# A two-layer hybrid trunk: w_ada sums, bias adds and half-tile norms put at other places of the queues

## The chip, the cores and the metric

One core of one Trainium2 chip runs the whole kernel in one launch. The metric is the device time of an execution in microseconds (us). Five engines take part, each with a queue of its own that it works through in order: TensorE (PE, matrix products), VectorE (DVE), ScalarE (ACT), GpSimd (POOL) and SyncE (SP, which here only issues loads and stores).

## The reference

Two layers of a shared trunk over 256 context tokens and 256 latent tokens, width 1024. Per layer:

```python
sh1, sc1, gt1, sh2, sc2, gt2 = split(silu(c) @ w_ada[l] + b_ada[l], 6)      # for latent and for context
h = rms_norm(x, g_attn[l]) * (1 + sc1) + sh1
p = h @ w_in[l]                                  # gates 2048 | c_q 768 | c_kv 256 | k_r 32 | NA q, k, v 3 x 512
mq = rms_norm(c_q, g_qa) @ w_uq[l]               # 8 heads x 96
kv = rms_norm(c_kv, g_kva) @ w_ukv[l]            # 8 heads x (64 + 64)
mq, mk = rms_norm(mq, g_mq), rms_norm([k_nope, k_r], g_mk)   # and a 2-D rope on 32 of the 96 for latent tokens
y_mla = softmax(mq mk^T / sqrt(96)) v            # context and latent keys
y_na = neighbourhood attention (window, position bias rpb) + context keys, one softmax
y = (sigmoid(g_a) * (y_mla @ w_mla_o) + sigmoid(g_b) * (y_na @ w_na_o)) @ w_out
x = x + gt1 * y
h2 = rms_norm(x, g_mlp[l]) * (1 + sc2) + sh2
x = x + gt2 * (relu(h2 @ w_ff1[l]) ** 2 @ w_ff2[l])
```

Context tokens read only context tokens; in the last layer only the latent stream goes on past the mixer. All is float32; the output is the latent stream.

## The kernel before, in words

**Products in three passes.** Every weight tile and every activation is split into a high part that the fast matmul takes exactly and a low rest. `wsplit` (L124) does it for weights: SP loads a raw tile of 512 KB (`wraw`, L116, five buffers "raw"), ACT writes `whi` (L127), DVE writes `wlo` as raw minus whi (L128); three buffers of each. `mm3` (L100) then gives three matmuls a product: hi x hi (L101), and the two mixed ones (L102, L103). `proj_a` (L131) makes an output tile of 128 features by up to 512 tokens out of 8 slices of depth, 24 matmuls; `proj_b` (L553) makes token tiles, two tokens blocks at a time, in a pair of banks. PSUM banks are A (2), B (3), C (2) and D (1).

**Modulation.** The six vectors of `w_ada` are needed by two streams (latent, context) and no matmul makes them: `ada_side` (L233) loads a slice of 128 rows by 1024 columns, multiplies it by one number of silu(c) per row and adds it to an accumulator on DVE, once per stream (L246 the first slice, L248 the other seven), then transposes and reduces (L259, L260), and one small matmul and four adds (L266, L270) finish it. A generator yields after each slice, and `step(n)` (L165) takes n slices wherever the kernel's author has put a call. `ada(l, j)` is vector j of layer l; j = 2 is the first gate, 3 and 4 shift and scale of the MLP norm, 5 its gate. Here (0, 2) is made beside w_uq, (0, 4) and (0, 3) beside the neighbourhood chunks and the attention behind them, the rest beside the MLP of layer 0.

**Stages of a layer**, in the order of PE's queue: the latent products c_q and c_kv with their norms; w_uq in three blocks of heads (288, 288 and 192 columns, L715 copies, L597 squares); w_ukv in two (L732, L733); the first gates (`gates`); MLA attention head by head; six chunks `chunk_na` (L959) for the neighbourhood q, k and v; neighbourhood attention with more gates between; the branch products and their merge (L1041 gates, L1045 and L1047 m and its low part, on POOL for six of eight tiles); w_out (`last_product`, L1068); the MLP in groups of eight tiles, `ff1` (L1137) and `ff2` (L1177). The norm between two stages is `rms_a` (L306: a matmul with ones, DVE's ms L316, POOL's rt L177), `rms_b` (L321: the factors spread over a bank, L324) and `norm_apply` (L330: per slice u on DVE L334, the high part on ACT L338, the low on DVE L340). `proj_tail` (L150) makes the last tiles before a norm in two halves, one per stream, so that the first half's norm runs under the second.

**Small statistics.** `q_stat` and `k_stat` (L692, L705) turn sums of squares into factors on POOL, for one block of 128 tokens at a time; the position bias comes with four small loads per table on SP (L809) and an add of the window mask on POOL (L810).

**Order.** The code records all of it in one order; a list scheduler of the language then gives each engine a fixed list by its own estimate of times and by the order of the program, and marks such as `keep_in_program_order` pin single instructions. What an engine's list says is therefore fixed before the run.

Of the kernel before, what the change touches and what calls it, by code (L numbers as in the profile page):

```python
# [45 lines left out]
def trunk(ctx: ExitStack, tc, t):
# [186 lines left out]
    def ada_side(parts, acc):  # L233


        for l, j, zs in parts:
            accs = [acc(z) for z in zs]
            for k in range(KD):
                raw = wraw(t["w_ada"][l], k, 1, j * D, D)[:, 0]
                for z, tiles in zip(zs, accs):  # L240
# [216 lines left out]
    for l in range(DEPTH):  # L457
# [149 lines left out]
        def rope(z, tab, lt, n):  # L607
# [8 lines left out]
            for i in range(2):  # L616
                nc.gpsimd.tensor_tensor(out=zz[:, :, :, i], in0=aa[:, :, :, i], in1=bb[:, :, :, 1 - i], op=ALU.add)
# [63 lines left out]
        if l == 0:  # L681
# [3 lines left out]
            step(2)  # L685
# [616 lines left out]
```

## Time and profile before

| what | us |
|---|---|
| median of 3 runs | 1317.86 (1313.06 to 1319.54) |
| the profiled execution | 1316.76 |
| its span, first to last instruction | 1315.0 |
| PE busy | 1276.4 (97%) |
| weight loads into PE | 1094.9 (83%) |
| DVE busy | 903.5 (69%) |
| ACT busy | 582.6 (44%) |
| POOL busy | 269.7 (21%) |
| mean granted clock of PE | 0.992 of 2.4 GHz |

The busy time of PE counts from a matmul's start to its modelled end, and neighbours overlap. In a timeline row the columns are start, duration, engine, line, operation, output tile <- input tiles, shapes, how many in a row, and in brackets the idle time just before it with what ended it. The shares hide where a stage waits; for that the gaps of PE are read one by one.

### The profile page before, as it was taken

To read this page: it belongs to the slowest core of one execution; us is meant where nothing else is said; L and a number is where in the kernel's file an instruction comes from. 1 tells how busy PE (TensorE), PEld (TensorE's weight loads), DVE (VectorE), ACT (ScalarE), POOL (GpSimd) and SP (SyncE) were. 2 spreads that over 40 slices of the span, in tenths; PEclk is the share of its full clock that TensorE was granted. 3 is DMA by queue.
4 is the path that set the end of the run, shared out by engine and by line. 5 is a ranking of instruction groups with operands and counts; after the bars stand their busy time and mean duration, and the time that the engine had idled before them with its cause. 6 is when DMAs were issued, how large, how long until landed. Compare 5 with 4: busy or idle time off the path is not lost.

```text
span 1315.0 us, 20278 instructions
## 1 busy us (share of the span) xinstructions
PE 1276.4 (97%) x7783; PEld 1094.9 (83%) x7783; DVE 903.5 (69%) x1545; ACT 582.6 (44%) x1052; POOL 269.7 (21%) x283
## 2 busy tenths in 40 slices
PE   7989999999999999999999999989999999999997
PEld 5788888986787898888888888889889789999896
DVE  4588387758985597997775665756763967665553
ACT  4445376446423334322323313455654545554452
POOL 0325501421004003210201100038122112121011
PEclk9999999999999999999999999999999999999999
DMA  9865500544495336566675572476214657656652
GB/s 290 298 147 148 174 17 17 180 134 57 114 321 182 114 111 179 169 182 195 205 224 176 160 224 85 120 176 182 77 49 113 134 171 211 175 159 194 192 183 90
DMA packets 241857, 208.01 MB, mean 158 GB/s; under 512 B 24464, under 2 KB 220816, under 8 KB 241376
## 3 DMA queue, kind: packets, MB, share of 16 engines
q1 hardware_dynamic: 231728, 190.16, 50.3%
q10 hardware_dynamic: 9520, 16.29, 3.5%
q8 instruction: 61, 1.00, 0.3%
q0 software_dynamic: 512, 0.27, 0.1%
q14 instruction: 36, 0.29, 0.1%
HBM read 195.15 MB, written 11.53 MB: 157 GB/s over the span
## 4 chain that ended last, share of the span: by engine, by line
PE 55%; DVE 3%; DMA 2%; ACT 1%; POOL 1%; issue 1%; POOLq 0%; ACTq 0%; DVEq 0%
PE psB L101 7%; PE psB L103 7%; PE psB L102 7%; PE psA L103 6%; PE psA L101 6%; PE psA L102 6%; PE psC L103 4%; PE psC L101 4%; PE psC L102 4%; PE psC L865 1%; DVE wlo L128 1%; PE psD L885 1%; ACT whi L127 1%; DMA raw<-in_w_uq_dram 1%; DMA bias<-in_rpb_dram 1%
## 5 line engine op out<-in xcount | busy, mean ns | idle before, releaser
L128 DVE TENSOR_TENSOR wlo<-raw,whi 128x1024 fp32r<-128x1024 f32 (+3 forms) x252 | 308.5, 1226 | 190.9 <-ACT whi L127 185.4
L127 ACT ACTIVATE whi<-raw 128x1024 fp32r<-128x1024 f32 (+3 forms) x252 | 260.4, 1035 | 364.1 <-PE psB L102 113.8
L248 DVE SCALAR_TENSOR_TENSOR ada<-raw,silu,ada 128x1024 f32<-128x1024 f32 (+1 forms) x126 | 153.1, 1245 | 25.5 <-DMA raw<-in_w_ada_dram 25.2
L102 PE MATMUL psA<-wlo,h 128*128 128x256 f32 (+2 forms) x408 | 121.1, 297 | 2.5 <-DVE wlo L128 2.5
L101 PE MATMUL psA<-whi,h 128*128 128x256 f32 (+2 forms) x408 | 120.8, 296 | 1.2 <-ACT h L338 1.1
L103 PE MATMUL psA<-whi,h 128*128 128x256 f32 (+2 forms) x408 | 120.9, 296 | 0.0
L101 PE MATMUL psB<-h,whi 128*128 128x512 f32 (+1 forms) x288 | 99.1, 345 | 0.1
L103 PE MATMUL psB<-h,wlo 128*128 128x512 f32 (+1 forms) x288 | 99.0, 344 | 0.0
L102 PE MATMUL psB<-h,whi 128*128 128x512 f32 (+1 forms) x288 | 99.0, 344 | 0.0
L101 PE MATMUL psA<-h,whi 128*128 128x512 f32 (+1 forms) x248 | 87.8, 355 | 0.8 <-ACT h L338 0.8
L103 PE MATMUL psA<-h,wlo 128*128 128x512 f32 (+1 forms) x248 | 87.3, 352 | 0.0
L102 PE MATMUL psA<-h,whi 128*128 128x512 f32 (+1 forms) x248 | 87.1, 351 | 0.0
L102 PEld LDWEIGHTS psA<-wlo,h 128*128 128x128 f32 x408 | 78.4, 192 | 5.6 <-DVE wlo L128 3.1
L101 PEld LDWEIGHTS psA<-whi,h 128*128 128x128 f32 x408 | 78.1, 192 | 3.4 <-ACT h L338 1.6
L103 PEld LDWEIGHTS psA<-whi,h 128*128 128x128 f32 x408 | 78.2, 192 | 1.9
L1156 POOL TENSOR_TENSOR fl<-s,fa 128x512 fp32r<-128x512 f32 (+1 forms) x32 | 36.2, 1130 | 167.0 <-ACT fa L1155 167.0
L101 PE MATMUL psC<-G,whi 128*128 128x258 f32 (+2 forms) x216 | 69.2, 321 | 0.3 <-ACT G L338 0.3
L102 PE MATMUL psC<-G,whi 128*128 128x258 f32 (+2 forms) x216 | 69.1, 320 | 0.2
L103 PE MATMUL psC<-G,wlo 128*128 128x258 f32 (+2 forms) x216 | 68.8, 319 | 0.2 <-DVE wlo L128 0.2
L1156 POOL TENSOR_TENSOR h<-s,h 128x512 fp32r<-128x512 f32 (+1 forms) x32 | 34.5, 1077 | 168.3 <-ACT h L1155 150.0
L102 PEld LDWEIGHTS psB<-h,whi 128*128 128x128 f32 x288 | 54.6, 190 | 6.8 <-issue 0.8
L101 PEld LDWEIGHTS psB<-h,whi 128*128 128x128 f32 x288 | 54.6, 190 | 6.9 <-issue 0.4
(389 smaller groups left out, 3323.7 us busy)
## 6 DMA issues: line engine op xcount, KB each, us to landing
raw<-in_w_ff_dram SPq DMA_DIRECT2D x128, 512.0 KB, 4.1
raw<-in_w_ada_dram SPq DMA_DIRECT2D x80, 512.0 KB, 4.1
raw<-in_w_in_dram SPq DMA_DIRECT2D x62, 512.0 KB, 3.7
raw<-in_w_out_dram SPq DMA_DIRECT2D x16, 512.0 KB, 4.5
spare<-in_w_ada_dram SPq DMA_DIRECT2D x12, 512.0 KB, 8.6
xT_d<-xT SPq DMA_DIRECT2D x2, 2048.0 KB, 10.2
bias<-in_rpb_dram SPq DMA_DIRECT2D x64, 64.0 KB, 7.0
g_d<-g ACTq DMA_DIRECT2D x16, 256.0 KB, 4.4
```

The source lines that it names most:

```text
L101: nc.tensor.matmul(out, sh, mh, start=first, stop=False)
L102: nc.tensor.matmul(out, sh, ml, start=False, stop=False)
L103: nc.tensor.matmul(out, sl, mh, start=False, stop=last)
L127: nc.scalar.activation(out=hi, in_=src, func=AF.Copy)
L128: nc.vector.tensor_tensor(out=lo, in0=src, in1=hi.bitcast(F32), op=ALU.subtract)
L248: nc.vector.scalar_tensor_tensor(out=a, in0=raw[:, c:c + w], scalar=sc, in1=a, op0=ALU.mult, op1=ALU.add)
L865: nc.tensor.transpose(o[:, kt * 256 + i * 128:kt * 256 + (i + 1) * 128], pt[:, (kp * 2 + kt) * 128:(kp * 2 + kt + 1) * 128], perm if K == ...
L885: mm = nc.tensor.matmul(yo[z * 64:(z + 1) * 64, oc], vsel(kt, 2 * hp + z), tr[kt // 2][:, kt % 2, :], start=kt == nkt - 1, stop=kt == 0, t ...
L1156: nc.gpsimd.tensor_tensor(out=al[:, f, :], in0=s[:, :TQ], in1=ah[:, f, :].bitcast(F32), op=ALU.subtract)
```

## The change

It does seven things.

- `ada_side` puts each of its sums behind an instruction that it names (`issue_after`): the low split of the last weight that the program has split by then, or, for the parts beside the MLP, the last step of the second stream's MLP norm.
- The two slices at w_uq's start and one per pair of token blocks in it are no longer taken there; w_ada of (0, 2) is taken in w_ukv and the gates, its rest after the gates.
- The bias adds on POOL are put behind the last rope on q.
- `q_stat` and `k_stat` work on two token blocks at once.
- `chunk_na` takes two slices after each of its six chunks, of (0, 4) alone.
- (0, 3), the shift of the MLP norm, is made beside merge and w_out. Its two sums stand in a new tile "fm"; the MLP's low parts of odd groups, 4096 wide in one tile "fl", become two tiles of 2048, fl and fm (`Halves`).
- Tails: three tiles instead of two are made in halves, hooks sit earlier, the first half's norm is done for slices 0 to 4 and 5 to 7 apart; in the first MLP group one slice is taken instead of three.

```diff
+class Halves:
+    def __init__(self, *tiles):
+        self.tiles = tiles
+    def __getitem__(self, i):
+        p, k, *r = i
+        n = self.tiles[0].shape[1]
+        return self.tiles[k // n][(p, k % n, *r)]
...
+    split = []
     def wsplit(src, k, n):
...
-        nc.vector.tensor_tensor(out=lo, in0=src, in1=hi.bitcast(F32), op=ALU.subtract)
+        split[:] = [nc.vector.tensor_tensor(out=lo, in0=src, in1=hi.bitcast(F32), op=ALU.subtract).ins]
...
-    def ada_side(parts, acc):
+    def ada_side(parts, acc, behind=None):
...
                 raw = wraw(t["w_ada"][l], k, 1, j * D, D)[:, 0]
+                lead, behind = behind or (lambda: split[0]), None
...
-                            nc.vector.tensor_scalar(out=a, in0=raw[:, c:c + w], scalar1=sc, scalar2=None, op0=ALU.mult)
+                            with tc.issue_after(lead()):
+                                nc.vector.tensor_scalar(out=a, in0=raw[:, c:c + w], scalar1=sc, scalar2=None,
+                                                        op0=ALU.mult)
...
         def ckv_hook(k):
-            if k == 4:
+            if k == 3:
                 nxt.append(rms_a(nxt[2], both[1][1], "C", True))
-            if k == 7:
-                nxt[3](1, rms_b(*nxt[4], True))
+            if k == 6:
+                nxt[3](1, rms_b(*nxt[4], True), range(KD))
...
             side.append(ada_side(((0, 2, (0, 1)),), lambda z: [ap.tile([128, TT], F32, tag="P", name="ada", bufs=4)
                                                                for _ in range(2)]))
-            step(2)
...
-        def q_stat(tk):
-            fin_r(qrs[:, tk, :], qrs[:, tk, :], QK)
-            nc.gpsimd.tensor_scalar(out=qrs[:, tk, :], in0=qrs[:, tk, :], scalar1=rq[:, tk - q0:tk - q0 + 1],
-                                    scalar2=0.0, op0=ALU.mult, op1=ALU.add)
+        def q_stat(t):
+            z = qrs[:, t:t + 2, :]
+            fin_r(z.rearrange("p t h -> p (t h)"), z.rearrange("p t h -> p (t h)"), QK)
+            nc.gpsimd.tensor_tensor(out=z, in0=z, in1=rq[:, t - q0:t - q0 + 2].unsqueeze(2).to_broadcast([128, 2, NH]),
+                                    op=ALU.mult)
...
                 head_ss(qrs[:, tk, h0:h0 + n], dst, n, QK, rq[:, tk - q0:tk - q0 + 1])
-                if h0 == 6:
-                    q_stat(tk)
-                if tk % 2:
-                    step()
+                if h0 == 6 and tk % 2:
+                    q_stat(tk - 1)
...
-        step(99)
         for tk in range(4):
             k_fin(tk)
         for tk in range(q0, 4):
-            q_fin(tk)
+            q_end = q_fin(tk)
 
         gates(NG0[l], "B")
+        step(99)
...
-                nc.gpsimd.tensor_tensor(out=bias.rearrange("p a i j -> p (a i) j"),
...
+                with tc.issue_after(q_end.ins):
+                    nc.gpsimd.tensor_tensor(out=bias.rearrange("p a i j -> p (a i) j"),
...
             proj_b(loader(w_in, 0, OFF_NA + part * 512 + half * 256, 256, 4, 8), 2, H, Lo, toks, 256, evac, "one")
-            if (part, half) in ((0, 1), (2, 0), (2, 1)):
-                step(2)
+            step(2)
...
-            side.append(ada_side(((0, 4, (0, 1)), (0, 3, (0, 1))), acc_v))
+            side.append(ada_side(((0, 4, (0, 1)),), acc_v))
...
-        y1l = po.tile([128, 8 * TQ], F32R, tag="fl", name="y1l", bufs=1)[:, :2048].rearrange("p (k n) -> p k n", k=4)
+        y1l = po.tile([128, 2048], F32R, tag="fl", name="y1l", bufs=1).rearrange("p (k n) -> p k n", k=4)
+        if l == 0:
+            spl = po.tile([128, 2048], F32, tag="fm", name="spl", bufs=1)
+            side.append(ada_side(((0, 3, (0, 1)),), lambda z: [spl[:, z * D:(z + 1) * D]]))
...
-                if (s_, i, k) == (1, 1, 0):
+                if (s_, i, k) == (1, 0, 7):
                     Rs.append(rms_a(acc, both[0][1], "D", True))
-                if (s_, i, k) == (1, 1, 5):
-                    then(rms_b(*Rs[0], True))
-
-            proj_a(w, k0, KD, 0, 6, moves, loc, res_add(gate, sq))
-            proj_tail(w, k0, (6, 7), moves, both, ev, hook)
+                if (s_, i, k) == (1, 1, 4):
+                    then(rms_b(*Rs[0], True), range(0, 5))
+
+            proj_a(w, k0, KD, 0, 5, moves, loc, res_add(gate, sq))
+            proj_tail(w, k0, (5, 6, 7), moves, both, ev, hook)
+            then(Rs[0][0], range(5, 8))
...
-            if f == 1:
+            if (f, k) == (1, 0):
                 R2.append(rms_a(Rs, both[1][1], "C", True))
-            if f == 2:
-                norm_2(1, rms_b(*R2[0], True))
+            if (f, k) == (1, 5):
+                R2.append(norm_2(1, rms_b(*R2[0], True), range(KD)))
...
-                al = po.tile([128, 8 * TQ], F32R, tag="fl", name="fl", bufs=1).rearrange("p (k n) -> p k n", k=8)
+                al = Halves(*(po.tile([128, 2048], F32R, tag=x, name="fl", bufs=1)
+                              .rearrange("p (k n) -> p k n", n=TQ) for x in (("fl", "fm") if l == 0 else ("fl",))))
...
                 for f, o in enumerate(os):
                     ev(f, o)
-                    step()
+                step()
...
-                                  (1, 3, (1,)), (1, 5, (1,))), acc_g))
+                                  (1, 3, (1,)), (1, 5, (1,))), acc_g, lambda: R2[1].ins))
```

The lists at the three places of which the prediction speaks. A row is the line, the operation, output <- inputs, the shape and how many follow each other; line numbers are 12 to 24 higher in the changed file.

DVE, layer 0, from w_uq's last blocks into w_ukv, in the changed kernel (`ada` are the w_ada sums of (0, 2), `qrs` and `krr` reductions of squares, `mqk` the copies out of w_ukv's banks):

```order
L142 TENSOR_TENSOR wlo<-raw,whi 128x1024
L617 TENSOR_REDUCE qrs<-sq 128x3
L262 TENSOR_SCALAR ada<-raw,silu 128x512 x4
L266 SCALAR_TENSOR_TENSOR ada<-raw,silu,ada 128x512 x4
L617 TENSOR_REDUCE qrs<-sq 128x2 x2
L142 TENSOR_TENSOR wlo<-raw,whi 128x1024
L266 SCALAR_TENSOR_TENSOR ada<-raw,silu,ada 128x512 x6
L617 TENSOR_REDUCE qrs<-sq 128x2
L266 SCALAR_TENSOR_TENSOR ada<-raw,silu,ada 128x512 x2
L617 TENSOR_REDUCE qrs<-sq 128x2
L142 TENSOR_TENSOR wlo<-raw,whi 128x1024
L750 COPY mqk<-psB 128x4x64 x2
```

Before, all sums of (0, 2) stood ahead of w_ukv's first split, between w_uq's; now the first two slices stand after that split and two more after the second.

DVE, layer 0, from the last MLA head (`PT`) into the neighbourhood chunks, before:

```order
L871 COPY PT<-psC 128x512
L246 TENSOR_SCALAR ada<-raw,silu 128x1024 x2
L248 SCALAR_TENSOR_TENSOR ada<-raw,silu,ada 128x1024
L128 TENSOR_TENSOR wlo<-raw,whi 128x1024
L248 SCALAR_TENSOR_TENSOR ada<-raw,silu,ada 128x1024
L598 TENSOR_REDUCE nrs<-sq 128x4 x2
L128 TENSOR_TENSOR wlo<-raw,whi 128x1024
```

and in the changed kernel (the second split of the chunk before stands earlier now, within the MLA attention):

```order
L890 COPY PT<-psC 128x512
L262 TENSOR_SCALAR ada<-raw,silu 128x1024 x2
L266 SCALAR_TENSOR_TENSOR ada<-raw,silu,ada 128x1024 x6
L617 TENSOR_REDUCE nrs<-sq 128x4 x4
L266 SCALAR_TENSOR_TENSOR ada<-raw,silu,ada 128x1024 x4
L142 TENSOR_TENSOR wlo<-raw,whi 128x1024 x2
```

Before, two sums of a pair stood ahead of the first split; now twelve instructions of (0, 4) do, and the split is that of the third chunk.

POOL, layer 1, around w_uq: `rt` is the factor of c_q's norm, `ro` the rope. Before:

```order
L617 TENSOR_TENSOR kr<-ro 128x2x8 x2
L810 TENSOR_TENSOR bias<-bias,wmask 128x512 x3
L177 TENSOR_TENSOR rt<-ms,mhalf 128x2
L613 TENSOR_TENSOR ro<-mqk,ropeq 128x256
```

and in the changed kernel:

```order
L636 TENSOR_TENSOR kr<-ro 128x2x8 x2
L191 TENSOR_TENSOR rt<-ms,mhalf 128x2
L632 TENSOR_TENSOR ro<-mqk,ropeq 128x256
L633 TENSOR_TENSOR ro<-mqk,ropeq 128x256
L636 TENSOR_TENSOR mqk<-ro 128x8x2x8 x2
L632 TENSOR_TENSOR ro<-mqk,ropeq 128x256
L633 TENSOR_TENSOR ro<-mqk,ropeq 128x256
L636 TENSOR_TENSOR mqk<-ro 128x8x2x8 x2
L829 TENSOR_TENSOR bias<-bias,wmask 128x512 x3
L620 TENSOR_SCALAR qrs<-qrs 128x16
L829 TENSOR_TENSOR bias<-bias,wmask 128x512
```

Three bias adds stood ahead of rt and one further up; now all four stand behind both ropes, among the statistics of q.

## Rows read from the trace of the kernel before

**Rows 1.** The page, busy time of the engines.

```profile
PE 1276.4 (97%) x7783; PEld 1094.9 (83%) x7783; DVE 903.5 (69%) x1545; ACT 582.6 (44%) x1052; POOL 269.7 (21%) x283
```

**Rows 2.** Timeline of PE, layer 0, w_uq from its start to w_ukv's.

```profile
78.32 0.51 PE L101 MATMUL psB<-whi,G 128*128 128x288 f32 x2
90.24 0.40 PE L101 MATMUL psA<-whi,G 128*128 128x288 f32 x1 [1.40 <-ACT mqk L715]
94.44 0.61 PE L102 MATMUL psB<-wlo,G 128*128 128x288 f32 x1 [3.80 <-DVE wlo L128]
113.77 0.42 PE L101 MATMUL psB<-whi,G 128*128 128x512 f32 x1
```

**Rows 3.** Timeline of ACT and of DVE, layer 0, w_uq.

```profile
86.00 0.93 ACT L127 ACTIVATE whi<-raw 128x864 fp32r<-128x864 f32 x1 [5.10 <-DMA raw<-in_w_uq_dram]
...
93.33 2.02 DVE L128 TENSOR_TENSOR wlo<-raw,whi 128x864 fp32r<-128x864 f32 x2
```

**Rows 4.** Windows: stretch, length; busy us (records) per engine; PE clock; DMA share, GB/s.

```profile
92.30:99.00 6.70, 4.57 (x19) 4.57 (x20) 6.70 (x11) 0.68 (x1) 0.00 (x0) 0.50 0.63 208
230.00:247.30 17.30, 15.49 (x126) 14.99 (x124) 14.10 (x16) 9.99 (x18) 6.70 (x6) 1.00 0.50 153
386.00:427.00 41.00, 39.54 (x172) 31.93 (x171) 24.20 (x29) 11.41 (x14) 16.58 (x12) 1.00 0.67 233
884.20:890.90 6.70, 6.29 (x30) 6.13 (x29) 4.65 (x7) 4.27 (x8) 0.00 (x0) 0.50 0.76 209
891.70:902.00 10.30, 10.30 (x48) 8.49 (x47) 7.41 (x15) 7.22 (x17) 9.46 (x13) 1.00 0.38 107
```

**Rows 5.** Timeline of PE, ACT and POOL, layer 1, w_uq.

```profile
883.98 0.39 PE L101 MATMUL psB<-whi,G 128*128 128x192 f32 x1 [3.79 <-ACT whi L127]
891.71 0.42 PE L101 MATMUL psA<-whi,G 128*128 128x512 f32 x1
...
882.52 0.54 ACT L597 ACTIVATE sq<-mqk,rt 128x288 f32<-128x288 f32 x1 [7.05 <-POOL rt L177]
...
880.56 1.26 POOL L810 TENSOR_TENSOR bias<-bias,wmask 128x512 f32<-128x512 f32 x1 [6.28 <-DMA bias<-in_rpb_dram]
```

**Rows 6.** Timeline of DVE and PE, layer 0, the neighbourhood chunks.

```profile
230.22 1.42 DVE L246 TENSOR_SCALAR ada<-raw,silu 128x1024 f32<-128x1024 f32 x2 [2.15 <-PE psD L885]
231.55 1.28 DVE L248 SCALAR_TENSOR_TENSOR ada<-raw,silu,ada 128x1024 f32<-128x1024 f32 x1
232.75 1.22 DVE L128 TENSOR_TENSOR wlo<-raw,whi 128x1024 fp32r<-128x1024 f32 x1
...
234.02 0.39 PE L102 MATMUL psA<-wlo,h 128*128 128x256 f32 x1 [0.42 <-DVE wlo L128]
247.35 0.39 PE L102 MATMUL psA<-wlo,h 128*128 128x256 f32 x1 [1.44 <-DVE wlo L128]
```

**Rows 7.** Branch products, 386 to 427: timeline of PE; DVE by line.

```profile
399.86 0.50 PE L103 MATMUL psC<-ym,wlo 128*128 128x512 f32 x1 [1.46 <-DVE wlo L128]
...
L128 DVE TENSOR_TENSOR wlo<-raw,whi 128x1024 fp32r<-128x1024 f32 x8 | 11.1, 1411 | 1.0 <-ACT whi L127 1.0
```

**Rows 8.** Timeline of DVE and PE, from layer 0 to layer 1.

```profile
812.04 1.24 DVE L260 TENSOR_REDUCE red<-ada 128x16 f32<-128x512 f32 x2
832.77 1.28 DVE L340 SCALAR_TENSOR_TENSOR h<-u,modT,h 128x256 fp32r<-128x256 f32 x3
...
837.93 0.40 PE L102 MATMUL psA<-wlo,h 128*128 128x288 f32 x1 [0.64 <-DVE wlo L128]
840.37 0.71 PE L324 MATMUL psC<-ident,rt 128*128 128x128 f32 x4 [0.39 <-POOL rt L177]
```

**Rows 9.** Timeline of DVE, layer 0, w_uq's end and w_ukv.

```profile
108.04 3.39 DVE L248 SCALAR_TENSOR_TENSOR ada<-raw,silu,ada 128x512 f32<-128x512 f32 x5
111.35 1.22 DVE L128 TENSOR_TENSOR wlo<-raw,whi 128x1024 fp32r<-128x1024 f32 x1
117.06 0.75 DVE L732 COPY mqk<-psB 128x256 f32<-128x256 f32 x2
```

More of the change, by code (lines that the diff above doesn't have):

```diff
@@ L245, in ada_side @@
                         if k == 0:
-                            nc.vector.tensor_scalar(out=a, in0=raw[:, c:c + w], scalar1=sc, scalar2=None, op0=ALU.mult)
-                        else:
-                            nc.vector.scalar_tensor_tensor(out=a, in0=raw[:, c:c + w], scalar=sc, in1=a,
-                                                           op0=ALU.mult, op1=ALU.add)
+                            with tc.issue_after(lead()):
+                                nc.vector.tensor_scalar(out=a, in0=raw[:, c:c + w], scalar1=sc, scalar2=None,
+                                                        op0=ALU.mult)
+                        else:
+                            with tc.issue_after(lead()):
+                                nc.vector.scalar_tensor_tensor(out=a, in0=raw[:, c:c + w], scalar=sc, in1=a,
+                                                               op0=ALU.mult, op1=ALU.add)
                         c += w
@@ L616, in rope @@
             for i in range(2):
-                nc.gpsimd.tensor_tensor(out=zz[:, :, :, i], in0=aa[:, :, :, i], in1=bb[:, :, :, 1 - i], op=ALU.add)
+                r = nc.gpsimd.tensor_tensor(out=zz[:, :, :, i], in0=aa[:, :, :, i], in1=bb[:, :, :, 1 - i], op=ALU.add)
+            return r
         kvss = ap.tile([128, 4], F32, name="kvss")
@@ L699, in q_fin, with k_stat @@
             if tk >= 2:
-                rope(z, ropeq[:, l], tk - 2, NH)
+                return rope(z, ropeq[:, l], tk - 2, NH)
             else:
-                nc.gpsimd.tensor_tensor(out=z, in0=z, in1=gqr[:, l, :].unsqueeze(1).to_broadcast([128, NH, RD]),
+                return nc.gpsimd.tensor_tensor(out=z, in0=z, in1=gqr[:, l, :].unsqueeze(1).to_broadcast([128, NH, RD]),
                                         op=ALU.mult)
-        def k_stat(tk):
-            ss = krr[:, tk, :]
-            nc.gpsimd.tensor_scalar(out=ss, in0=ss, scalar1=krs[:, tk:tk + 1], scalar2=0.0, op0=ALU.add, op1=ALU.add)
-            fin_r(krr[:, tk, :], ss, QK)
-            nc.gpsimd.tensor_scalar(out=krz[:, tk, :], in0=krr[:, tk, :], scalar1=rk[:, tk:tk + 1], scalar2=0.0,
-                                    op0=ALU.mult, op1=ALU.add)
+        def k_stat(t):
+            z = krr[:, t:t + 2, :]
+            nc.gpsimd.tensor_tensor(out=z, in0=z, in1=krs[:, t:t + 2].unsqueeze(2).to_broadcast([128, 2, NH]), op=ALU.add)
+            fin_r(z.rearrange("p t h -> p (t h)"), z.rearrange("p t h -> p (t h)"), QK)
+            nc.gpsimd.tensor_tensor(out=krz[:, t:t + 2, :], in0=z,
+                                    in1=rk[:, t:t + 2].unsqueeze(2).to_broadcast([128, 2, NH]), op=ALU.mult)
         for h0, n in ((0, 3), (3, 3), (6, 2)):
@@ L734, in evac @@
                 head_ss(krr[:, tk, hs], dst, 4, NOPE, rs)
-                if hf == 1:
-                    k_stat(tk)
+                if hf == 1 and tk % 2:
+                    k_stat(tk - 1)
                 if tk % 2:
```

28 lines of the change are left out of this document (15 added, 13 removed).

## Prediction

> **What bounds the kernel now.** I read the busy shares first, then every idle gap of TensorE (PE) with its releaser, then the granted clock of the stretches around the longest gaps, and last what stood on the engine that released them. PE is busy 97% of the span [rows 1], so the kernel is one long queue of matmuls, and a change can only win the gaps in it (1315.0 - 1276.4 = 38.6 us, the start-up among them, which the change leaves alone) and the slow stretches behind them. Four places matter.
>
> Dip A, layer 0, w_uq: PE waits 1.40 us for ACT's copies and 3.80 us for a wlo on VectorE (DVE) [rows 2]. ACT had stood 5.10 us on the load of that weight, which SP had issued behind w_ada rows, and DVE put its two splits behind w_ada sums, at 93.33 [rows 3]. Until 99 the clock is then at the lower of its two levels, 1.2 instead of 2.4 GHz (0.50 in the table) [rows 4]: of the stretch from 94.44 on, half, 2.3 us, is lost.
>
> Dip C, layer 1, w_uq: 3.79 us [rows 5]. ACT's square of q waited 7.05 us for GpSimd's (POOL) rt, which ran only behind a bias add that had waited 6.28 us for its table, until 880.56; ACT's next weight split stood behind that square. The clock is at 0.50 from 884 to 891 [rows 4].
>
> At the neighbourhood chunks PE waits 0.42 and 1.44 us for wlo [rows 6]; at the branch products 1.46 us [rows 7]; at the layer boundary 0.64 and 0.39 us [rows 8].
>
> **The change, part by part.** *Dip C.* The bias adds now stand behind the last rope on q, so rt follows ms at once. w_uq's last 36 matmuls ended at 891.71 after PE had stopped at 880.19: 11.5 us. At half clock one takes 6.29/30 = 0.21 us [rows 4], at full clock 0.11, so 4.0 us for all: gain **7.5** (at least 6.5, should a load or split still bind for 1 us). What POOL gets behind the ropes, four bias adds at 1.3 us, lies under the eight gate products that PE runs next (192 matmuls of 256 columns at 0.12, 23 us). With pairs it has fewer instructions there; if that cover failed, the price would be the adds, 5 us.
>
> *Dip A.* SP issues all six w_uq loads without a w_ada row between them, and no w_ada sum stands ahead of w_uq's splits. Of the 35.45 us from 78.32 to 113.77 [rows 2], 5.2 of waits and 2.3 of slow clock go: w_ukv starts at 106.3 instead of 113.77. Gain 7.5.
>
> But the same 64 half-row sums now stand in w_ukv and the gates. DVE's list is fixed: 8 sums, 2 reductions, one split, 6 sums, a reduction, 2 sums, a reduction, one split, and only then the first copy out of w_ukv's banks. The list can begin when DVE has reduced the squares of w_uq's second block. That product ends 72 short matmuls (8 us) before 106.3; two copies, two squares and a split on ACT follow (0.93 for a split [rows 3], in all some 3 us): 101.5. From there, by [rows 9]: 16 sums at 0.66 (3.39 for five) are 10.6, four reductions at 0.3 (a copy of that size is 0.37) 1.2, two splits 2.3, together 14.1: the copy stands at 115.6 to 116, and ends with ACT's copy behind it at 116.8. PE has five banks for these tiles and uses the sixth time, the first bank again, after 27 matmuls at 10.30/48 = 0.215 us [rows 4]: it wants it at 106.3 + 5.8 = 112.1. **New wait: 4.5 us**, in the middle of w_ukv. The lower clock followed both waits of this length (rows at 92.30 and 884.20); for it I take 2.0 (0 if the clock holds, 3 if it lasts as there). Dip A: -7.5 + 4.5 + 2.0 = **-1.0** (-3.0 to +0.5).
>
> *The neighbourhood chunks, layer 0.* Their w_ada sums need tile "v", which is free when the last MLA mix ends, 230.22 [rows 6], called E. Before, splits stood between the sums. Now 2 multiplies, 6 sums, 4 reductions and 4 sums stand ahead of the third chunk's first wlo, and four of the five raw buffers hold w_ada rows through the attention, so that chunk's own load starts only when the sums free one. DVE: 1.33 + 6 x 1.2 + 1.3 + 4 x 1.2 + 1.13 (pair, sum and split as 230.22, 231.55 and 232.75 follow each other) = 15.8; the last two reductions wait about 1.2 for the squares of the chunk before: E + 17. PE has 65 matmuls until then, at 15.49/126 = 0.123 us [rows 4] E + 8. **New wait: 9.0 us** for 1.86 that go: +7.1 net, and 1.5 for the clock (0 to 3, since part of a slow stretch lies in the wait): **+8.6** (+6.5 to +10.5). Later chunks find their splits done 4 us ahead.
>
> *Branch products and w_out, layer 0.* Here 14 sums and 2 multiplies of a whole row (18.1 us) are new. DVE is busy 24.2 of 41.0 us [rows 4]; with its list worked through in order, each wlo still stands some 3 us ahead of its first matmul. The 1.46 us wait came from POOL's and ACT's order of m and h, which now alternate: **-1.0** (-1.5 to +5, below). The transposes that leave the end of the attention gave no wait there.
>
> [rows 7] hold a hint against that sum: a wlo takes 1411 ns in this stretch, beside POOL's m and h, against 1222 elsewhere [rows 9]. The Trainium skill (SBUF — State Buffer, "Who interferes with whom" and "SBUF: two separate sides") says that a VectorE instruction with two SBUF inputs and a GpSimd instruction take one port pair in turn, as an exclusive lock. By that page the new sums, which have two such inputs, would be slowed and would slow POOL here; by the row alone I add nothing to the likeliest sum. The result that it would give is the third rival.
>
> *Layer boundary.* The last w_ada part finishes later: two transposes, a reduction and a second reduction (0.6 each, 1.24 for two [rows 8]) now stand ahead of the 576-column wlo and of ms. From rms_b on, DVE has 16 norm steps at 0.40 (1.28 for three), two residual adds and two sums (1.5), an 864 split 1.0 [rows 3], three of these ada steps 1.9 and the split 0.7: 11.5 plus 0.25 to start. PE is there after 36 + 36 matmuls at 0.12 and 0.13, 9.1: wait 2.6 instead of 0.64. Behind it reduction, four adds, ms and rt delay rms_b by 1.1 instead of 0.39. +2.6, and 0.7 for a longer slow stretch: **+3.3** (+2 to +5.5).
>
> *The rest.* A third tile is done in halves, twice: 48 pairs of 256 columns for one of 512, by the averages of [rows 4] 0.03 us each, 1.5 in all; since some records are missing from the shorter ones, +0.4. The halved fl tile, hooks a step earlier, one w_ada step in the first MLP group instead of three: PE's queue covers them, 0, and 1 us if a norm step slips.
>
> **Sum:** -7.5 - 1.0 + 8.6 - 1.0 + 3.3 + 0.4 = +2.8 on the profiled run's 1316.8: 1319.6. That run lies 1.1 below the median of the runs shown, so the median should be about **1320.7**. Against 1317.86 that is no change: 0.5% (6.6 us) is about what a measurement of this kernel can tell from none.
>
> **The rivals.** (1) *The waits come, the clock holds, and PE loses only them.* -7.5 - 3.0 + 7.1 - 1.5 + 2.6 + 0.4 = -1.9: 1316. For it: a gap of 1.44 us left the clock at 1.00 [rows 4, 6]; against: both gaps of 3.8 did not. Chance 0.2. (2) *The two old dips go and the new waits do not end last*, because DVE reaches the sums earlier than I think: -7.5 - 7.5 - 1.9 - 1.5 + 0.4 = -18: 1300. Against: an engine takes its list in order, and the sums at E cannot start before the mix. Chance 0.1. (3) *Slower: the branch products become DVE's.* 24.2 + 18.1 = 42.3 for 41.0; if each of the 14 sums stretches by the 0.19 us that a wlo shows, 44.9; PE then waits 3.9 and loses about 1 to the clock: +5 instead of -1.0, 1326.7. It decides from the point where DVE is busy for all of that stretch. The SBUF page speaks for it. Chance 0.25. (4) *The bias move does not free rt*, the add's wait going over to q's and k's statistics and from there to the first transposes: of the 7.5 some 4 come back, 1325. The table came by 880.56, ten us before the add now asks for it; chance 0.05.
>
> **How the numbers follow.** My forecast has 0.4. Faster by over 0.5% (below 1311.3): all of (2), a seventh of (1), 0.05 of the forecast: 0.16, rounded up to 0.18 for waits I priced too long. Slower (above 1324.4): 0.85 of (3), a fifth of the forecast, half of (4): 0.31, say 0.30. Within: 0.52. Range: the low ends of A, the chunks and the boundary together give 1315; the two new waits at half my price (-6.8) and without a slow clock (-3.5) give 1310; the high end of the chunks on top of (3) gives 1329. (2) is left out: 1310 to 1329.
>
> **What would show it.** Right: no wait on ACT at w_uq in both layers; a PE wait of 4 to 5 us inside w_ukv of layer 0 released through a DVE copy; one of 8 to 10 us at the third neighbourhood chunk, released by wlo; 2 to 3 us in the boundary's ckv products. Wrong: no PE gap over 2 us between 100 and 260 (then rival 2), DVE without idle in the branch products (rival 3), or POOL's bias add still ahead of rt.

## The result and the profile after

The changed kernel takes **1323.07 us** (median of 7 runs, 1320.14 to 1324.42), the kernel before 1315.34 in the same comparison (7 runs, 1313.06 to 1319.54): a ratio of **1.0056**, 95% interval 1.0039 to 1.0072. The prediction said 1320.7, range 1310 to 1329, with "no change within 0.5%" the likeliest (0.52). The time is in the range, 2.4 us above the forecast; the loss of 0.56% lies just outside that 0.5%, with an interval that reaches to both sides of it. The profiled execution of the changed kernel takes 1320.14 with a span of 1318.4 us, 3.4 more than before's; the sum on record was +2.8.

The page, PE's share ([rows 1] before): the number of matmuls rose by the 48 of the halved tile, and PE's busy time did not.

```profile
PE 1275.3 (97%) x7831; PEld 1095.2 (83%) x7831; DVE 909.5 (69%) x1547; ACT 582.6 (44%) x1054; POOL 262.2 (20%) x258
```

The timeline of PE in the changed kernel, its longer waits from 100 us on that were not there before or grew (what ended a wait stands in brackets):

```profile
117.36 0.80 PE L113 MATMUL psB<-whi,G 128*128 128x512 f32 x1 [4.92 <-ACT mv L751]
...
243.37 0.39 PE L113 MATMUL psA<-whi,h 128*128 128x256 f32 x1 [1.44 <-ACT whi L141]
...
250.91 0.58 PE L114 MATMUL psA<-wlo,h 128*128 128x256 f32 x1 [6.61 <-DVE wlo L142]
...
426.82 0.50 PE L115 MATMUL psA<-ym,wlo 128*128 128x512 f32 x1 [0.77 <-DVE wlo L142]
...
441.08 0.49 PE L113 MATMUL psB<-h,whi 128*128 128x512 f32 x1 [1.07 <-ACT h L1067]
442.21 0.50 PE L114 MATMUL psB<-h,whi 128*128 128x512 f32 x1 [0.63 <-DVE h L1068]
...
848.31 0.40 PE L114 MATMUL psA<-wlo,h 128*128 128x288 f32 x1 [2.37 <-DVE wlo L142]
851.13 1.22 PE L342 MATMUL psC<-ident,rt 128*128 128x128 f32 x4 [0.56 <-POOL rt L191]
```

Neither w_uq shows a wait of over 0.3 us any more: dips A and C [rows 2, 5] are gone. In their place stand a wait in w_ukv, one at the third neighbourhood chunk in two pieces (PE waits for whi, runs a few matmuls, waits for wlo) and one of 2.37 us at the boundary, as listed under "what would show it". The pair at 441, in the first tile of w_out, was not.

Windows of the changed kernel (columns as in [rows 4]): behind the two long waits PE runs at half clock (0.50), at w_out it keeps the full one in this execution, and layer 1's w_uq now runs all at full clock.

```profile
117.30:120.10 2.80, 2.73 (x7) 2.16 (x8) 2.80 (x7) 2.51 (x8) 2.72 (x5) 0.50 0.92 273
...
250.90:256.00 5.10, 5.09 (x24) 5.09 (x25) 5.10 (x5) 1.06 (x1) 0.00 (x0) 0.50 0.91 270
441.00:446.00 5.00, 4.29 (x18) 3.33 (x19) 5.00 (x8) 1.72 (x3) 0.00 (x0) 1.00 0.16 47
...
884.20:894.60 10.40, 10.40 (x86) 10.40 (x86) 5.21 (x8) 5.70 (x12) 0.39 (x1) 1.00 0.80 188
```

The stages, in us, each from its first matmul to that of the next, read from the timelines of PE. Three of the experiments below stand beside them: e3 is the changed kernel with fewer sums at the neighbourhood chunks, e7 the changed kernel with the sums moved at three places, e11 the kernel before with the bias adds moved and the statistics in pairs:

| stage | before | after | e3 | e7 | e11 |
|---|---|---|---|---|---|
| start to w_uq, layer 0 | 78.3 | 78.5 | 81.4 | 77.7 | 78.3 |
| w_uq, layer 0 | 35.5 | 27.6 | 27.6 | 27.6 | 33.2 |
| w_ukv, layer 0 | 11.2 | 17.5 | 18.2 | 10.9 | 11.2 |
| gates to the last neighbourhood chunk's last matmul | 155.3 | 164.2 | 153.4 | 155.8 | 155.0 |
| from there to the branch products | 100.4 | 100.8 | 100.5 | 100.1 | 100.4 |
| branch products | 46.5 | 46.2 | 46.2 | 46.2 | 46.6 |
| w_out and the MLP, layer 0 | 404.7 | 406.0 | 407.5 | 406.0 | 404.6 |
| boundary, to w_uq of layer 1 | 38.0 | 39.7 | 39.7 | 33.7 | 36.6 |
| w_uq, layer 1 | 21.9 | 14.2 | 14.2 | 14.2 | 14.4 |
| from there to PE's last instruction | 415.9 | 416.4 | 416.4 | 417.8 | 415.9 |

What held w_ukv's first copy is the list that [rows 9] priced. DVE's timeline, changed kernel, with two rows of POOL beside it:

```profile
101.66 1.67 DVE L262 TENSOR_SCALAR ada<-raw,silu 128x512 f32<-128x512 f32 x4
103.24 3.70 DVE L266 SCALAR_TENSOR_TENSOR ada<-raw,silu,ada 128x512 f32<-128x512 f32 x4
...
107.38 1.21 DVE L142 TENSOR_TENSOR wlo<-raw,whi 128x1024 fp32r<-128x1024 f32 x1
108.52 4.05 DVE L266 SCALAR_TENSOR_TENSOR ada<-raw,silu,ada 128x512 f32<-128x512 f32 x6
...
108.75 3.27 POOL L191 TENSOR_TENSOR qrs<-qrs,mhalf 128x16 f32<-128x16 f32 x1
...
112.76 2.26 DVE L266 SCALAR_TENSOR_TENSOR ada<-raw,silu,ada 128x512 f32<-128x512 f32 x2
113.29 1.18 POOL L633 TENSOR_TENSOR ro<-mqk,ropeq 128x256 f32<-128x256 f32 x1
...
115.20 1.21 DVE L142 TENSOR_TENSOR wlo<-raw,whi 128x1024 fp32r<-128x1024 f32 x1
116.33 0.41 DVE L750 COPY mqk<-psB 128x256 f32<-128x256 f32 x1
...
233.98 1.42 DVE L262 TENSOR_SCALAR ada<-raw,silu 128x1024 f32<-128x1024 f32 x2 [2.15 <-PE psD L904]
235.31 7.26 DVE L266 SCALAR_TENSOR_TENSOR ada<-raw,silu,ada 128x1024 f32<-128x1024 f32 x6
...
244.86 4.86 DVE L266 SCALAR_TENSOR_TENSOR ada<-raw,silu,ada 128x1024 f32<-128x1024 f32 x4
249.64 2.35 DVE L142 TENSOR_TENSOR wlo<-raw,whi 128x1024 fp32r<-128x1024 f32 x2
```

It begins at 101.66 (forecast 101.5) and the copy stands at 116.33 (115.6 to 116); PE stopped at 112.44 (112.1). Four multiplies and twelve sums are the 16 that were priced. From 233.98 on, the chunk's list: two multiplies, six sums, four sums, and then the split ([rows 6] had splits between them).

### The profile page after: what moved, and what is told of

It reads as the page before. It is cut to its first block, busy times and chain, and to the rows that moved or that the text cites. A ratio compares the mean times of both kernels' runs of the same rounds, so it can differ in the third digit from the quotient of the medians.

```text
span 1318.4 us, 20363 instructions
## 1 busy us (share of the span) xinstructions
PE 1275.3 (97%) x7831; PEld 1095.2 (83%) x7831; DVE 909.5 (69%) x1547; ACT 582.6 (44%) x1054; POOL 262.2 (20%) x258
## 4 chain that ended last, share of the span: by engine, by line
PE 55%; DVE 3%; POOL 2%; ACT 1%; DMA 1%; issue 1%; POOLq 0%; ACTq 0%; SPq 0%; DVEq 0%
PE psB L113 7%; PE psB L114 7%; PE psB L115 7%; PE psA L113 6%; PE psA L115 6%; PE psA L114 6%; PE psC L115 4%; PE psC L114 4%; PE psC L113 4%; DVE wlo L142 1%; PE psC L884 1%; PE psD L904 1%; ACT whi L141 1%; DMA raw<-in_w_in_dram 1%; PE psB L938 1%
## 5 line engine op out<-in xcount | busy, mean ns | idle before, releaser
L266 DVE SCALAR_TENSOR_TENSOR ada<-raw,silu,ada 128x1024 f32<-128x1024 f32 (+1 forms) x112 | 138.7, 1270 | 0.2
L113 PE MATMUL psB<-h,whi 128*128 128x256 f32 (+1 forms) x272 | 91.9, 339 | 1.2 <-ACT h L1067 1.1
L114 PE MATMUL psB<-h,whi 128*128 128x256 f32 (+1 forms) x272 | 91.9, 338 | 0.6 <-DVE h L1068 0.6
L115 PE MATMUL psB<-h,wlo 128*128 128x256 f32 (+1 forms) x272 | 91.7, 337 | 0.0
L1180 POOL TENSOR_TENSOR h<-s,h 128x512 fp32r<-128x512 f32 (+1 forms) x32 | 38.1, 1191 | 168.5 <-ACT h L1179 151.1
L113 PE MATMUL psB<-G,whi 128*128 128x512 f32 (+2 forms) x192 | 66.8, 348 | 0.0
L115 PE MATMUL psB<-G,wlo 128*128 128x512 f32 (+2 forms) x192 | 66.3, 345 | 0.3 <-DVE wlo L142 0.3
L114 PE MATMUL psB<-G,whi 128*128 128x512 f32 (+2 forms) x192 | 66.4, 346 | 0.0
L113 PE MATMUL psC<-G,whi 128*128 128x258 f32 (+2 forms) x200 | 62.6, 313 | 0.0
L114 PE MATMUL psC<-G,whi 128*128 128x258 f32 (+2 forms) x200 | 62.5, 312 | 0.0
```

Of the source, the lines that this page charges most:

```text
L113: nc.tensor.matmul(out, sh, mh, start=first, stop=False)
L114: nc.tensor.matmul(out, sh, ml, start=False, stop=False)
L115: nc.tensor.matmul(out, sl, mh, start=False, stop=last)
L1180: nc.gpsimd.tensor_tensor(out=al[:, f, :], in0=s[:, :TQ], in1=ah[:, f, :].bitcast(F32), op=ALU.subtract)
```

## The experiments

**e0_again**, unedited. 

> The changed kernel once more, unedited. The ledger theory (two new waits in layer 0 and a longer one at the boundary, the old dips gone): again 1320 to 1325 us, ratio to the kernel before 1.004 to 1.008; gaps of about 4.9 us in w_ukv and 8 us at the third neighbourhood chunk in its trace. Rival (part of the loss in the first comparison was the chip's drift): ratio within 1.000 to 1.003.

Measured: 1322.83 us (1321.76 to 1324.54), ratio 1.0057 (1.0038 to 1.0075). So the loss is real, and the profiled run of the first comparison was a short one. This second trace has a span of 1322.8, mean clock 0.988, where the first had 0.991; the same waits, 4.92, 1.60 with 6.62, 1.07 with 0.63. Its windows show where the extra time went: half clock for longer in w_ukv, and a slow clock at 20 us (the start-up, which the change leaves alone) and behind the waits at w_out; at these two the first trace has 1.00.

```profile
119.90:124.00 4.10, 4.07 (x10) 3.24 (x11) 4.10 (x8) 3.71 (x8) 3.94 (x6) 0.50 0.60 187
...
20.00:25.00 5.00, 4.21 (x26) 3.04 (x27) 4.35 (x14) 2.71 (x6) 0.00 (x0) 0.68 1.01 338
...
443.40:448.40 5.00, 4.36 (x11) 3.23 (x12) 5.00 (x8) 1.69 (x2) 0.00 (x0) 0.66 0.15 43
```

**e2_gates**, fewer sums ahead of w_ukv's copies:

```diff
-                if tk % 2:
+                if hf == 1 and tk % 2:
                     step()
...
-        gates(NG0[l], "B")
+        for _ in range(NG0[l]):
+            gates(1, "B")
+            step()
```

> The changed kernel with the layer-0 sums of (0, 2) taken out of the first half of w_ukv; two steps stay in the second half, and one stands behind each of the six gate products. Theory (the w_ukv wait is the copy standing behind 16 sums): the gap of 4.9 us and the 1.4 us of slow clock behind it go, and the gates' splits keep their lead: 6 us less than the changed kernel. Rival (VectorE has too much to do in that stretch wherever the sums stand): the wait moves to a gate's wlo, at most 2 us less.

Measured: 1323.15 us, ratio 1.0057 (1.0038 to 1.0076), no gain: the rival. The edit did more than its expectation says: the projection of a gate already makes one step of its own, so each gate now had two. PE and DVE, e2_gates:

```profile
114.56 0.79 PE L113 MATMUL psB<-whi,G 128*128 128x512 f32 x1 [2.21 <-ACT mv L751]
136.17 0.80 PE L115 MATMUL psB<-h,wlo 128*128 128x512 f32 x1 [3.34 <-DVE wlo L142]
...
127.29 7.67 DVE L266 SCALAR_TENSOR_TENSOR ada<-raw,silu,ada 128x512 f32<-128x512 f32 x8
```

With half the sums ahead of the copy its wait is halved, and the eight in a row between two gates' splits give the rest back at a gate: 2.21 + 3.34 for 4.92. These eight take 0.96 us each, where the six at 108.52 above took 0.68.

**e8_less_pool**, e2_gates with less on POOL:

```diff
-            if tk >= 2:
+            if tk >= 2 and l:
                 return rope(z, ropeq[:, l], tk - 2, NH)
...
-            nc.gpsimd.tensor_tensor(out=z, in0=z, in1=krz[:, tk, :]...
+            if l:
+                nc.gpsimd.tensor_tensor(out=z, in0=z, in1=krz[:, tk, :]...
```

> e2_gates with less for GpSimd to do in layer 0: the rope on q's image tokens is left out (they get the gain alone), and so is the product of k with its statistics; all sums of w_ada stay where they are. Theory (a sum with two operands in SBUF is stretched while GpSimd multiplies whole tiles): the eight sums between the second and third split of the gates, 7.67 us there, take 5.3 to 5.8, and the gate's wlo wait of 3.34 us falls to 1 to 2. Rival (they wait for their rows, or take that long by themselves): they stay above 7 us.

Measured (one run, 1321.21 us): DVE and POOL, e8_less_pool:

```profile
113.89 2.02 DVE L142 TENSOR_TENSOR wlo<-raw,whi 128x1024 fp32r<-128x1024 f32 x1
...
128.39 6.10 DVE L266 SCALAR_TENSOR_TENSOR ada<-raw,silu,ada 128x512 f32<-128x512 f32 x8
...
111.42 5.62 POOL L832 TENSOR_TENSOR bias<-bias,wmask 128x512 f32<-128x512 f32 x3
```

The eight sums take 6.10 instead of 7.67 (a little above the 5.3 to 5.8 expected; POOL still writes k there), and the gate's wait falls from 3.34 to 0.51; another of 1.23 comes at the next gate. The bias adds, freed of the ropes, came forward to 111.42, and now the split beside them takes 2.02 instead of 1.21, so that w_ukv's wait grew from 2.21 to 3.84, and the run is no shorter than the traced one of e2_gates (1321.16). The rival falls: the sums are stretched by what POOL does beside them.

**e3_late_chunks:**

```diff
-            step(2)
+            if (part, half) in ((0, 1), (2, 0), (2, 1)):
+                step(2)
```

> The changed kernel with the steps at the neighbourhood chunks only behind the last three chunks, as in the kernel before; the reductions of (0, 4) then fall after the attention's gates. Theory (the third chunk waits because all 12 sums and its load's buffer come first): the gaps of 1.4 and 6.6 us go, 0 to 2 us come at later chunks, and the slow clock behind them goes: 6 to 8 us less than the changed kernel. Rival (the sums only move on and hold chunks four to six): 0 to 2 us less, with a wlo wait of over 4 us between 245 and 270 us.

Measured: 1312.30 us (12 runs, 1310.80 to 1314.16), ratio 0.9977 (0.9965 to 0.9989): 10.5 less than e0_again on the same chip, more than expected. PE has no wait of over 0.44 us between 220 and 320 us; the stage of the chunks takes 153.4 for 164.2, two less than in the kernel before, since the waits of [rows 6] are gone too. Here two multiplies and two sums stand ahead of the split at 251.51 and cost nothing; the twelve ahead of the split at 249.64 in the changed kernel cost all of it.

**e4_three_steps:**

```diff
                     ev(f, o)
-                step()
+                    step()
```

> The changed kernel with a step behind each of the first three ff1 tiles instead of one behind all three, so that the last part of w_ada is done two steps earlier, before the boundary. Theory (at the boundary a transpose and a reduction stand ahead of the ckv split and of ms): the wait of 2.4 us shrinks to about 0.6 and rms_b's wait by 0.2: 1.5 to 2.5 us less than the changed kernel. Rival (the norm's 16 steps alone hold that split): no change, within 0.5 us.

Measured: 1328.92 us, ratio 1.0100 (1.0081 to 1.0119), 6 more than e0_again. The theory holds at its place, for the boundary takes 33.7 us instead of 39.7 and the wait of 2.37 is gone; but PE waits in the first ff1 group instead. PE and DVE, e4_three_steps:

```profile
509.02 0.50 PE L113 MATMUL psA<-G,whi 128*128 128x512 f32 x1 [1.43 <-ACT whi L141]
514.78 0.80 PE L115 MATMUL psB<-G,wlo 128*128 128x512 f32 x1 [5.02 <-DVE wlo L142]
...
511.25 1.27 DVE L266 SCALAR_TENSOR_TENSOR ada<-raw,silu,ada 128x1024 f32<-128x1024 f32 x1
512.44 2.28 DVE L142 TENSOR_TENSOR wlo<-raw,whi 128x1024 fp32r<-128x1024 f32 x1
```

With the slow clock behind it, w_out and the MLP take 418.2 for 407.5. That the change makes one step there instead of three is what keeps this wait away.

**e1_bias_alone**, the kernel before with one part of the change:

```diff
-                nc.gpsimd.tensor_tensor(out=bias.rearrange(...
+                with tc.issue_after(q_end.ins):
+                    nc.gpsimd.tensor_tensor(out=bias.rearrange(...
```

> The kernel before, with one part of the change alone: the bias adds are issued behind the last rope on q. Theory (layer 1's dip at w_uq is rt standing behind a bias add that waits for its table, and nothing else binds there): the wait of 3.79 us and the half clock behind it go, 7 to 8 us less than the kernel before (ratio about 0.9943). Rival (the add's wait goes over to the statistics of q and k, which in the changed kernel the pairs make up for): 3 us less or none, with a wait in w_ukv or at the first transposes of layer 1.

**e10_pairs_alone**, the kernel before with `q_stat` and `k_stat` of the change. 

> The kernel before with the statistics of q and k in pairs, and nothing else. Theory (pairs and bias move gain only together): rt still stands behind the bias add, the dip at layer 1's w_uq stays, 0 to 1 us less than the kernel before. Rival (fewer instructions on GpSimd bring the bias adds and rt forward by themselves): 3 us less or more.

**e11_bias_and_pairs**, both. 

> The kernel before with both: the bias adds behind the last rope on q, and the statistics in pairs. Theory: the dip at layer 1's w_uq goes and nothing comes at the first transposes of the attention: 7 to 8 us less than the kernel before (ratio 0.994 to 0.9947). Rival (the 5.0 us that bias_alone showed at the transposes come back here too, and it was another part of the change that kept them out): 3 us less or none.

Measured: the bias move alone 1319.59 us, ratio 1.0017 (1.0002 to 1.0032); the pairs alone 1315.57, 0.9992 (0.9977 to 1.0007); both **1310.36, 0.9943 (0.9924 to 0.9961)**. Alone neither gains. Together the medians fall by 6.3 us and the ratio gives 7.5; in the trace layer 1's w_uq falls by 7.5, the gain that the prediction gave to the bias move. PE and POOL, e1_bias_alone:

```profile
922.47 0.45 PE L781 MATMUL psC<-ident,mqk 128*96 128x128 f32 x1 [5.01 <-POOL mqk L746]
...
882.75 1.50 POOL L613 TENSOR_TENSOR ro<-mqk,ropeq 128x256 f32<-128x256 f32 x1 [10.73 <-ACT mqk L716]
...
921.37 1.04 POOL L746 TENSOR_TENSOR mqk<-mqk,krz 128x512 f32<-128x512 f32 x1
```

POOL in e11_bias_and_pairs, over the same work:

```profile
881.00 1.50 POOL L613 TENSOR_TENSOR ro<-mqk,ropeq 128x256 f32<-128x256 f32 x1 [9.84 <-ACT mqk L717]
...
914.68 0.61 POOL L749 TENSOR_TENSOR mqk<-kr,krr 128x256 f32<-128x256 f32 x1
```

With the bias add moved, rt no longer waits and w_uq falls from 21.9 to 15.1; but PE arrives at the attention that much sooner, and POOL needs 39.7 us from the first rope to the last k (882.75 to 922.41), the moved adds among them. PE waits 0.69 and 5.01 us for it. The pairs bring this to 34.3 (881.00 to 915.29), and the transposes wait 0.34 us for it. With the pairs alone the dip stays, 2.76 us at 884.

**e6_two_tiles:**

```diff
-                if (s_, i, k) == (1, 0, 7):
+                if (s_, i, k) == (1, 1, 0):
...
-            proj_a(w, k0, KD, 0, 5, moves, loc, res_add(gate, sq))
-            proj_tail(w, k0, (5, 6, 7), moves, both, ev, hook)
-            then(Rs[0][0], range(5, 8))
+            proj_a(w, k0, KD, 0, 6, moves, loc, res_add(gate, sq))
+            proj_tail(w, k0, (6, 7), moves, both, ev, hook)
```

> The changed kernel with the last products (w_out and the last part of w_ff2) of layer 0 in halves for two tiles again, and their sums of squares and norms hooked where the kernel before has them. Theory (48 pairs of 256 columns cost 0.03 us each over one of 512): 0.5 to 1.5 us less, less whatever waits for rt and rms_b come back (0.9 us in the kernel before). Rival (the third tile in halves pays for itself by these waits): 0.5 us more or no change.

Measured: 1320.91 us, ratio 1.0040 (1.0026 to 1.0054). Against e0_again's 1.0057 the intervals overlap, so the total settles nothing. The stage of the boundary takes 37.9 us for the 39.7 of the changed kernel, but DVE's list there is another one too (below); e9 shows the other sign.

**e5_late_and_half** and **e7_late_and_none**, put together from what the runs had shown. Both have e3's edit and

```diff
-            step(4)
+            step(5 if g else 4)
```

in ff2 (two steps sooner at the boundary, without e4's burst); e5 has e2's first line too, without its second, and e7 has no step in w_ukv at all. 

> The changed kernel with the neighbourhood steps of e3_late_chunks, the steps of the first half of w_ukv taken out (each gate has one of its own), and one step more in each of two of the ff2 groups, so that the last part of w_ada is done before the boundary without more sums in the first ff1 group. Theory: e3's 10.5 us; in w_ukv 8 sums stand ahead of the first copy instead of 16 (4.9 us of wait become 1 to 2, the clock gives 1); at the boundary 2.4 become 0.6: 1305 to 1308 us. Rival (the sums beside GpSimd's ropes take 0.96 us instead of 0.67 and hold the gates' splits too): 1310 us or more.

> As e5_late_and_half, but with no step in w_ukv at all: the sums of (0, 2) begin in the gates and end behind them. Theory: no wait in w_ukv, 1303 to 1306 us. Rival (8 to 12 sums in a row stand ahead of a split that the attention or a gate wants): the wait comes back there, 4 us or more between 125 and 160 us, and the time is no better than e5_late_and_half.

Measured: e5 1305.82 us, ratio 0.9911 (0.9893 to 0.9930), as the theory had it; PE still waits 2.22 us in w_ukv, with 8 multiplies and sums ahead of the copy instead of 16. e7 **1300.43 us (1299.01 to 1303.57), ratio 0.9877 (0.9853 to 0.9900)**: 15 less than the kernel before, 22 less than the changed kernel. Its windows of w_ukv and of the boundary:

```profile
105.30:116.20 10.90, 10.90 (x51) 9.01 (x50) 9.88 (x20) 7.33 (x17) 10.59 (x12) 1.00 0.52 151
...
824.20:857.90 33.70, 32.81 (x258) 31.90 (x257) 28.52 (x59) 21.52 (x52) 5.67 (x11) 1.00 0.74 183
```

PE has no wait in w_ukv, the boundary keeps its clock, and the mean clock of the run is 0.999. The row of twelve sums that the rival feared is there (10.33 us from 136.94 on), and PE waits for none of the splits behind it.

**e9_best_two_tiles**, e7 with e6's edit. 

> e7_late_and_none with the last products in halves for two tiles again, as in e6_two_tiles. Theory (e6_two_tiles was 1.9 us shorter than the changed kernel in medians, since the third tile costs more than the waits that it saves): 0.5 to 2 us less than e7_late_and_none, 1298 to 1300 us. Rival (e6 gained by the boundary's waits, which e7 has no more): the same as e7 or up to 1 us more.

Measured: 1305.80 us (1303.51 to 1309.09), ratio 0.9919 (0.9902 to 0.9935), 5 more than e7. The rival, and more of it than expected: the boundary takes 36.7 instead of 33.7, with a wait of 0.65 there (and one of 1.11 for the norm's h, where e7 has 0.45). Two waits of PE, e9_best_two_tiles:

```profile
832.44 0.40 PE L114 MATMUL psA<-wlo,h 128*128 128x288 f32 x1 [0.65 <-DVE wlo L142]
...
1064.14 0.38 PE L113 MATMUL psB<-ym,whi 128*128 128x256 f32 x1 [1.93 <-ACT whi L141]
```

The MLP stage is no shorter with two tiles (406.6 against 406.0), so the halves of the third tile cost nothing that can be seen there, and at the boundary they gain 3.0 us. The last wait is in layer 1's branch products, where the edit changes nothing; the kernel before has 0.44 us there and e10 1.50. Why it varies was not tried.

## Why the prediction was right, and where its sum was off

The two long waits in layer 0 and the two dips that went are as forecast, in place, cause and size. The likeliest outcome, within 0.5%, was missed narrowly (1.0056 and 1.0057), and that the sum comes out so near (+2.8 against +3.4 in the traces) is in part luck: one term was 2.0 us too low, another 1.6 too high.

**Dip C, -7.5: right (21.9 to 14.2, -7.7), with its condition.** The text named the price if POOL's cover failed, 5 us, and that pairs shorten POOL's list; e1 shows a wait of just this size, 5.01, but not the whole price: with 0.69 ahead of it and a clock of 0.71 over the 7.6 us behind it, the stretch from w_uq's end on is 9.1 us longer (425.0 for 415.9). The gain belongs to both edits, and neither has it alone.

**Dip A, -7.5 + 4.5 + 2.0: right (-7.9, then +6.3 in w_ukv: 4.92 of wait, the rest half clock).** Two prices in it were wrong and nearly cancelled: the multiplies take 0.42 us and not 0.66, and the sums beside POOL's products and ropes 0.92 to 1.13. The words "the same 64 half-row sums" are a slip: there are 32, and the list that was summed holds the right 16. e5 and e7 show the mechanism by steps: 16 ahead of the copy 4.92 us, 8 ahead 2.22, none ahead none.

**The neighbourhood chunks, +8.6: right (155.3 to 164.2, +8.9).** PE asked at 241.9, 8 us behind E = 233.98, and had its split at 250.9, E + 17, both as worked out; 1.44 of the wait ends with the chunk's own load, which SP issued only at 237.82, behind the first sums, as the prediction had it. Two small errors cancel: PE ran 0.9 us of matmuls in between, so it waits 8.05 and not 9.0, and the clock behind costs some 2.6 (5.10 us at half) and not 1.5. e3 takes back 10.8 us of this stage.

**Branch products and w_out, -1.0: the wrong sign (-0.3 and +1.3).** The sums stretch, as the third rival had it, and by more than its 0.19 us, but over the stage DVE does not become the bound. Window, and DVE and POOL by line, changed kernel, 388.6 to 434.8 us; behind it the end of the stage alone:

```profile
388.60:434.80 46.20, 45.11 (x195) 35.77 (x193) 35.86 (x33) 12.37 (x15) 19.97 (x12) 1.00 0.63 198
L266 DVE SCALAR_TENSOR_TENSOR spl<-raw,silu,spl 128x1024 f32<-128x1024 f32 x13 | 20.8, 1617 | 0.0
L142 DVE TENSOR_TENSOR wlo<-raw,whi 128x1024 fp32r<-128x1024 f32 x7 | 9.3, 1325 | 5.5 <-ACT whi L141 5.5
L1066 POOL TENSOR_TENSOR m<-g 128x512 f32<-128x512 f32 x6 | 11.6, 1932 | 62.3 <-DVE g L1062 62.3
...
425.30:434.80 9.50, 8.71 (x38) 6.79 (x38) 9.50 (x8) 2.75 (x3) 4.15 (x3) 1.00 0.52 152
```

A sum takes 1617 ns, and POOL's m 1932 (1455 in the same stretch before), yet DVE is busy for 35.86 of 46.2 us and stands idle for 5.5 of the rest ahead of its splits, for ACT. The stage itself takes 46.2 for 46.5; the old wait of 1.46 is gone, and one of 0.77 stands at 426.82. What the step overlooked is the end of it: there DVE is busy without a gap, as the third rival had it for the whole stage, and the last tiles' g, m and lo are DVE's. The last g of the kernel before, and the last ones of the changed kernel:

```profile
427.36 0.69 DVE L1041 SCALAR_TENSOR_TENSOR g<-g,psC 128x512 f32<-128x512 f32 x1 [0.62 <-PE psC L103]
...
438.94 0.68 DVE L1062 SCALAR_TENSOR_TENSOR g<-g,psC 128x512 f32<-128x512 f32 x1
439.68 0.68 DVE L1066 TENSOR_TENSOR m<-g 128x512 f32<-128x512 f32 x1
440.28 1.30 DVE L277 STREAM_TRANSPOSE ada<-spl 128x512 f32<-128x512 f32 x2
441.50 0.65 DVE L1068 TENSOR_TENSOR h<-m,h 128x512 fp32r<-128x512 f32 x1
```

Before, DVE waited for the last product; now it takes it 4 us after PE's last branch matmul (434.52). So w_out's first tile waits 1.07 us for ACT's copy of m and 0.63 for lo, ahead of which the two transposes of the new sums stand as well. The stage of w_out and the MLP is longer by 1.3 in all, and by 2.8 in e0_again, where the clock falls there. The runs built on the kernel before, e1, e10 and e11, have neither wait and 404.6 us; no run moved these sums alone, so the cause is read from the timelines and not shown by an edit.

**Boundary, +3.3: too dear (+1.7), and two parts of the change priced apart that act together.** The split is late by 2.37 (2.6 forecast), rms_b by 0.56 (1.1 forecast). The stage in the runs, in us:

| last part of w_ada | two tiles in halves | three tiles in halves |
|---|---|---|
| late | 37.9 (e6) | 39.7 (changed kernel, e3) |
| in time | 36.7 (e9) | 33.7 (e4, e5, e7) |

With three tiles a late last part costs 6.0 us, and when it is in time the third tile in halves gains 3.0. The edit of e6 moves DVE's list too: its transposes and reductions (832.34) stand ahead of the stage and only the four adds fall into it, so what a late part costs with two tiles is not shown. The kernel before, with two tiles and in time, takes 38.0, and 36.6 once its bias adds are moved (e1, e11); the prediction had nothing for that.

**Halves, +0.4: no cost shown in the MLP's stage** (e9 406.6, e7 406.0); at the boundary they gain or lose with the last part of w_ada, as above.

**From the sum to the median.** The sum of +2.8 against +3.4 in the profiled runs is right; the step that turned it into a median was not. Before's profiled run was taken as 1.1 below its median and proved 1.4 above it (1315.34 over seven runs), and the changed kernel's is the shortest of its seven. Its other six have mean clocks of 0.986 to 0.990 (four of them 0.988) against 0.991; 0.003 of 1320 us is 4 us of work at full clock, about what they are longer by. The text said that half the clock follows a long wait; it did not say that the same wait costs a different amount from run to run, and the trace at hand was the cheapest of the seven. Rival 1 (the clock holds), rival 2 (no new waits) and rival 4 (rt stays behind the bias add) fall by the rows above; rival 3 (DVE the bound of the branch products) holds for the last 10 us of that stage alone. The 0.16 in the chances for "faster" should read 0.15; nothing hangs on it.

## What to carry to other kernels

When work is taken out of a place where it held the bound, price the place where it lands by the same list, instruction by instruction: here 15.6 us were won at the two w_uq stages, and 15.2 lost where w_ada's sums stood ahead of a copy or a split; moving only such sums, at three places (e7), kept the gain. What decides is what PE needs next behind the sums, and when, and not their number alone: eight cost 2.2 us ahead of w_ukv's copy (e5) and 3.3 ahead of a gate's split (e2), and twelve in a row cost nothing where PE did not yet want what stood behind them (e7). And an edit that shortens one engine's wait brings PE sooner to the next one, so two edits that do nothing alone may be worth measuring together.

## What was not expected of the hardware

A DVE sum of half a row took 0.68 us with POOL quiet or busy on 16 columns, and 0.92 to 1.13 beside POOL's products and adds; of a whole row 1.28, and 1.62 on average in the branch products, while POOL's own m rose from 1.46 to 1.93. Taking part of POOL's work away brought eight sums from 7.67 to 6.10 us (e2, e8). The Trainium skill (SBUF — State Buffer, "SBUF: two separate sides" and "Who interferes with whom") has this as a lock that one of the two holds for a whole instruction. The traces agree that both are slowed; the mean stretch in them is a quarter to two thirds of an instruction, and no run here shows whether one waits out a whole instruction of the other.

The granted clock does not follow from the wait alone: behind the same 1.07 and 0.63 us at w_out it stayed at 1.00 in one execution of the changed kernel and was 0.66 over 5 us in another. The seven executions of the changed kernel lie 4.3 us apart, with mean clocks of 0.986 to 0.991, and e7, with no wait of over 1.4 us behind the start-up, has the highest mean clock of all, 0.997 to 0.999.
